# Two half sums for gate and up at the start of a one-core encoder step, with a hand-set order of the first loads and instructions

## The chip, the cores and the metric

The kernel runs on one core of a Trainium2 chip. The metric is device time in microseconds for one execution. In the profile's words PE is TensorE's matmuls, PEld its weight loads, DVE is VectorE, ACT ScalarE, POOL GpSimd, and SP the queue that issues every DMA here.

## The reference

One layer of a streaming encoder is applied to 1024 prompt frames and 32 sample frames, each of 1024 features. The part that matters here is its beginning:

```
mod = silu(c) @ w_mod + b_mod                 # 9 pieces of 1024: shift, scale, gate for three sub-layers
h = rmsnorm(x, gains[0]) * (1 + sc1) + sh1
x = x + 0.5 * g1 * rmsnorm(swiglu(h, w1_gate, w1_up, w1_down), gains[1])
swiglu(h) = (silu(h @ w_gate) * (h @ w_up)) @ w_down          # inner width 2816
```

After it come two attention mixers (a chunk band with 8 heads, and a sliding window with sinks), their output projection, and a second feed-forward block of the first one's form. All is in float32.

## The kernel before

The 1056 frames are cut into three **token blocks** of 384, 384 and 288 columns; features lie on the partitions, in 8 tiles of 128 (`KT`). Every float32 matrix product is made in three: weights and activations are each split into a high part (rounded to fp32r) and the remainder, and `mm3` (lines 325 to 327) adds high x high, high x low and low x high. A weight tile is loaded raw into one of three buffers (`rpool`) and split by ACT (line 303) and DVE (line 304) into one of eight buffers (`wpool`).

The inner width of the feed-forward block is 22 **units** of 128 columns, taken two at a time. For each pair and each block `up` makes gate and up of a unit (2 x 24 products), then silu on ACT (line 550), the product on DVE (551), and the split of the result (553, 554). `down` makes 48 products of a pair into `dn` and adds them to `facc`. For block 0 of the first pair `down` follows at once, since nothing has been begun; then come block 1's gate and up.

Ahead of that stands the **start**. `load_x` fetches a block of x; `transpose_x` turns it by PE (line 617) into a two-bank PSUM buffer, of which there are two (`ps2`), and copies each half out, first DVE, then ACT (line 619). `mod_chunk(n)` loads 2 MB of `w_mod`, makes 512 columns of the modulation (line 186), copies them (`mr`, 189), transposes them (192), and `coefs` adds the bias and makes the scale (`acoef`, 207). Chunks 0 and 1 are the shift of features 0 to 511 and 512 to 1023, chunks 2 and 3 the scale of the same halves. `norm_h` squares x (364), adds up over the features (368, 370, then 357 on PE), takes a reciprocal root by three Newton steps (334 to 338), spreads it over the partitions by PE (`pr`, 405) and makes `h_hi` and `h_lo`. For block 0 (`ahead` is 4) x times the root is made before the coefficients are known (423), and shift and scale come with lines 440 to 442. For blocks 1 and 2 both are in one (420 and 444 to 449). The order in which these pieces are written is the string

```
START = "x02nw1y3"
```

(x a step of block 0, digits chunks, n its norm up to "ahead", w unit 0's gate and up weights, y the load of block 1's x). SP's queue keeps the written order up to the end of the first pair; the other engines' orders are set by a scheduler. Each engine runs its queue in order, so a waiting instruction holds up all that is behind it.

Two small things of later stages stand in the start too: the sinks' loads (lines 276 and 279) and the DVE steps `nsk` (282) and `es` (884) that read them. SP has eight lanes of DMAs, and each DMA waits for the one eight before it.

Of the kernel before, what the change touches and what calls it, by code (L numbers as in the profile page):

```python
# [16 lines left out]
D = 1024  # L17
KT = D // 128
# [36 lines left out]
INORDER = True  # L55
START = "x02nw1y3"
ROUNDS = {"h1": ((), 3), "h3": ((((0, 1), 2), ((2,), 2)), 0)}
# [17 lines left out]
def encoder_step(ctx: ExitStack, tc, x_prompt, x_sample, cache_a_k, cache_a_v, cache_b_k, cache_b_v,  # L75
# [39 lines left out]
    def p1(name, shape=(128, 512)):  # L115
        return ps1.tile(list(shape), F32, name=name, tag="p1")
# [181 lines left out]

    def split_w(src):
        r = rpool.tile([128, 8, 128], F32, name="raw", tag="r")  # L300
        dma.dma_start(r, src)
        w = wpool.tile([128, 2, 8, 128], F32R, name="w", tag="w")
        ae.activation(w[:, 0], r, AF.Copy)  # L303
        ve.tensor_sub(w[:, 1], r, w[:, 0])  # L304
        return w

    def split_cols(wm, c):
        return split_w(wm[0, :, 128 * c:128 * c + 128].rearrange("(k p) n -> p k n", p=128))

# [85 lines left out]

    def mean_rstd(src, kts, w, scale, ends, bank=None):

        bank = bank or pc
        pss = yield from sumsq(src, kts, w, bank, ends)
        y = rstd_cols(pss, w, scale)  # L400
# [100 lines left out]
    def need(key):  # L501
        while key not in done:
            step(1)

    def between(f, tb, j, H):
# [18 lines left out]

    def ffn(key, H, F, wg, wu, wd, per_group, key_out, after, beside=lambda ff, tb: None):
        late, pre = [], {}
# [6 lines left out]

        load(0, 0)
        yield
        for r, (gi, blocks) in enumerate(plan):
# [3 lines left out]
            def up(ff, tb):  # L540
                need((key, tb))
                w = TB[tb][1]
                hi, lo = H[tb]
                ps = [p1("gate"), p1("up")]
                for s in range(2):
                    for k in range(KT):
                        mm3(ps[s][:, :w], wgu[ff][s], k, hi[:, k, :], lo[:, k, :], k == 0, k == KT - 1)
                    step(FAST if gi == 0 else PACE)
                sl = s_tile([128, 384], "sl")
# [39 lines left out]
            if r:  # L589
                load(r, x)  # L590
            load(r, y)
            if r == XAT and key == "h1":
                XIN[1] = load_x(1)
            wgu.update({x: pre[r, x], y: pre[r, y]})
            for ff in grp:
                wds[ff] = split_rows(wd, ff)
            for tb in blocks:
# [41 lines left out]

    ffn1 = ffn("h1", H1, F1, w1_gate, w1_up, w1_down, mod_rest, "h2", lambda tb: between(F1[tb], tb, 0, H2))  # L640
    first = start(0)
    for o in START:
        if o == "x":
            next(first)
        elif o == "n":
            for said in first:
                if said == "ahead":
                    break
        elif o == "w":
            next(ffn1)  # L650
        elif o == "y":
            XIN[1] = load_x(1)
        else:
            mod_chunk(int(o))
    for tb in range(3):
        begin(("h1", tb), start(tb) if tb else first)
    for _ in ffn1:
# [698 lines left out]
```

## Time and profile before

| | |
|---|---|
| median of 3 runs | 2217.93 us (2214.45 to 2221.46) |
| the profiled execution | 2217.6 us, of which the span is 2215.8 |
| mean granted TensorE clock | 0.984 |
| PE busy | 2161.6 us, 98% of the span |
| PE busy in the first 45 us | 28.35 us |
| DVE busy, ACT busy | 1239.1 us, 697.8 us |
| DMA moved | 186.03 MB, 318 GB/s in the first 45 us |

The span is what the trace shows, from the first to the last instruction; 1.8 us lie around it. All times of rows are microseconds from the span's start. A timeline row has start, duration, engine, line, operation, output <- inputs, shapes, and in brackets the idle time before it and what ended it. A row "x4" holds four instructions. In a row of groups stand busy time, mean nanoseconds of one, and idle time before with its releasers. A matmul's own duration covers its passage through the array; the next one starts earlier, so the distance of two starts is what one costs in a row of them.

### The profile page before, as it was taken

The numbers are of one execution on the slowest core, as the hardware profiler recorded it, in microseconds if no ns is written. First come the engines' busy times: TensorE is split into PE (matmuls) and PEld (weight loads), VectorE is DVE, ScalarE is ACT, GpSimd is POOL, SyncE is SP. The second block draws the span as 40 slices with busy tenths as digits, with TensorE's granted clock in tenths as the row PEclk, the third lists the DMA queues.
The fourth block names the chain that finished last, engine by engine and source line by source line (L and its number), as shares of the span: only waits on it lengthen the run. The fifth ranks groups of instructions, "written<-read, shape, count | busy, mean of one in ns | idle before, by whom it ended". The sixth has DMA issues, their size and how long they took to land.

```text
span 2215.8 us, 33976 instructions
## 1 busy us (share of the span) xinstructions
PE 2161.6 (98%) x14012; PEld 2068.6 (93%) x14012; DVE 1239.1 (56%) x2425; ACT 697.8 (31%) x1450; POOL 179.2 (8%) x281
## 2 busy tenths in 40 slices
PE   6999999999999999899999899999999999999998
PEld 4999999999999999799787589999999999999998
DVE  5788667874333497677444865785333333333336
ACT  4411111111121253576444663542111111111133
POOL 1100000000000023001110313220000000000000
PEclk8999999999999999899999899999999999999999
DMA  9253334434122352111112121424211111111122
GB/s 323 93 153 118 111 96 124 143 101 129 39 66 69 101 184 93 38 39 30 50 30 62 46 77 67 134 86 120 66 58 39 57 39 39 58 38 58 39 69 79
DMA packets 200623, 186.03 MB, mean 84 GB/s; under 512 B 7597, under 2 KB 169813, under 8 KB 199317
## 3 DMA queue, kind: packets, MB, share of 16 engines
q1 hardware_dynamic: 200468, 183.87, 27.1%
q8 instruction: 110, 1.80, 0.3%
q14 instruction: 45, 0.36, 0.1%
HBM read 164.12 MB, written 22.86 MB: 84 GB/s over the span
## 4 chain that ended last, share of the span: by engine, by line
PE 90%; DVE 4%; DMA 3%; ACT 1%; issue 1%; POOL 0%; SPq 0%; ACTq 0%; DVEq 0%; POOLq 0%
PE dn L325 7%; PE dn L326 7%; PE dn L327 7%; PE gate L327 7%; PE gate L326 7%; PE up L327 7%; PE up L326 7%; PE gate L325 7%; PE up L325 7%; PE po L713 3%; PE S L752 2%; PE pq L325 2%; PE pq L327 2%; PE pq L326 2%; DMA raw<-in_w_gate_dram 1%; PE pp L776 1%
## 5 line engine op out<-in xcount | busy, mean ns | idle before, releaser
L326 PE MATMUL gate<-h_lo,w 128*128 128x384 f32 (+1 forms) x1056 | 340.2, 322 | 4.0 <-DVE h_lo L446 4.0
L325 PE MATMUL dn<-gg,w 128*128 128x384 f32 (+1 forms) x1056 | 341.4, 325 | 1.1 <-DVE facc L581 1.0
L581 DVE TENSOR_TENSOR facc<-dn,facc 128x768 f32<-128x768 f32 (+1 forms) x240 | 212.9, 889 | 230.2 <-PE dn L327 229.9
L326 PE MATMUL dn<-gg,w 128*128 128x384 f32 (+1 forms) x1056 | 340.6, 323 | 0.6 <-DVE gg L554 0.6
L325 PE MATMUL gate<-h_hi,w 128*128 128x384 f32 (+1 forms) x1056 | 341.0, 323 | 0.0
L327 PE MATMUL gate<-h_hi,w 128*128 128x384 f32 (+1 forms) x1056 | 340.4, 322 | 0.0
L325 PE MATMUL up<-h_hi,w 128*128 128x384 f32 (+1 forms) x1056 | 340.2, 322 | 0.0
L326 PE MATMUL up<-h_lo,w 128*128 128x384 f32 (+1 forms) x1056 | 340.0, 322 | 0.0
L327 PE MATMUL dn<-gg,w 128*128 128x384 f32 (+1 forms) x1056 | 340.0, 322 | 0.0
L327 PE MATMUL up<-h_hi,w 128*128 128x384 f32 (+1 forms) x1056 | 339.9, 322 | 0.0
L304 DVE TENSOR_TENSOR w<-raw,w 128x1024 fp32r<-128x1024 f32 x187 | 231.5, 1246 | 150.5 <-ACT w L303 150.3
L303 ACT ACTIVATE w<-raw 128x1024 fp32r<-128x1024 f32 x187 | 195.7, 1056 | 266.1 <-PE dn L327 103.5
L550 ACT ACTIVATE sl<-gate 128x384 f32<-128x384 f32 (+1 forms) x132 | 60.9, 462 | 563.9 <-PE gate L327 560.9
L551 DVE TENSOR_TENSOR sl<-sl,up 128x384 f32<-128x384 f32 (+1 forms) x132 | 68.5, 519 | 292.1 <-PE up L327 286.1
L326 PEld LDWEIGHTS gate<-h_lo,w 128*128 128x128 f32 x1056 | 198.6, 188 | 4.6 <-DVE h_lo L446 4.6
L325 PEld LDWEIGHTS dn<-gg,w 128*128 128x128 f32 x1056 | 199.2, 189 | 1.6 <-DVE facc L581 1.2
L326 PEld LDWEIGHTS dn<-gg,w 128*128 128x128 f32 x1056 | 199.2, 189 | 1.0 <-DVE gg L554 0.9
L327 PEld LDWEIGHTS dn<-gg,w 128*128 128x128 f32 x1056 | 199.1, 189 | 0.0
L325 PEld LDWEIGHTS gate<-h_hi,w 128*128 128x128 f32 x1056 | 198.7, 188 | 0.1
L327 PEld LDWEIGHTS gate<-h_hi,w 128*128 128x128 f32 x1056 | 198.7, 188 | 0.0
L327 PEld LDWEIGHTS up<-h_hi,w 128*128 128x128 f32 x1056 | 198.7, 188 | 0.0
L325 PEld LDWEIGHTS up<-h_hi,w 128*128 128x128 f32 x1056 | 198.5, 188 | 0.0
(224 smaller groups left out, 3367.4 us busy)
## 6 DMA issues: line engine op xcount, KB each, us to landing
raw<-in_w_mod_dram SPq DMA_DIRECT2D x56, 512.0 KB, 4.0
raw<-in_w_gate_dram SPq DMA_DIRECT2D x54, 512.0 KB, 4.0
raw<-in_w_up_dram SPq DMA_DIRECT2D x54, 512.0 KB, 4.7
raw<-in_w_down_dram SPq DMA_DIRECT2D x54, 512.0 KB, 4.5
raw<-in_w_in_dram SPq DMA_DIRECT2D x18, 512.0 KB, 4.3
wm<-in_w_mod_dram SPq DMA_DIRECT2D x8, 1024.0 KB, 7.4
raw<-in_w_out_dram SPq DMA_DIRECT2D x13, 512.0 KB, 4.5
xr<-xs SPq DMA_DIRECT2D x16, 384.0 KB, 3.5
```

The source lines that it names most:

```text
L303: ae.activation(w[:, 0], r, AF.Copy)
L304: ve.tensor_sub(w[:, 1], r, w[:, 0])
L325: te.matmul(ps, w[:, 0, k], hi, start=start, stop=False)
L326: te.matmul(ps, w[:, 0, k], lo, start=False, stop=False)
L327: te.matmul(ps, w[:, 1, k], hi, start=False, stop=stop)
L550: ae.activation(sl[:, :w], ps[0][:, :w], AF.Silu)
L551: ve.tensor_tensor(sl[:, :w], sl[:, :w], ps[1][:, :w], op=OP.mult)
L581: ve.tensor_tensor(o, ps[:, :, :w], o, op=OP.add)
L713: te.matmul(po[64 * h:64 * h + 64, :n], vsl(j, h, kn), PT(h, j, kn), start=j == 0, stop=j == nt - 1)
L752: te.matmul(S[:, c:ce], self.T[:, h, :], KQ[:, 0, 128 * k0 + c:128 * k0 + ce], start=True, stop=True)
L776: te.transpose(pp[:, j - j0, :], P[:, 128 * j:128 * j + 128], ident)
```

## The change

Six things are done.

- `START` goes. In its place stands a hand-written order, inside a region in which PE, DVE and ACT keep the written order of the region's instructions. SP keeps it as before.
- Loading and using are taken apart: `mod_load` beside `mod_chunk`, `raw_w` beside `split_raw`.
- For block 0 and the first two units, gate and up are made in two halves of the features by `half_products`: features 0 to 511 as soon as chunks 0 and 2 are known, 512 to 1023 after chunks 1 and 3. Unit 0 has two `p1` banks for its sums, unit 1 one of the two `p2` buffers (`gu`). Within a half the three products of each feature tile are sorted by kind.
- Chunk 1 and unit 1's gate weights are loaded ahead of the sinks.
- The squares of block 0 aren't folded on POOL and DVE any more (`fold=not ahead`); PE adds up all eight tiles (24 small matmuls in place of 6).
- Block 1's transposes and the first pair's down weights are written at the end of the region.

```
+    def half_products(ps, ws, h, half):
+        w = TB[0][1]
+        hi, lo = h
+        ks = range(4 * half, 4 * half + 4)
+        for s in range(2):
+            for k in ks:
+                te.matmul(ps[s][:, :w], ws[s][:, 0, k], hi[:, k, :], start=k == 0, stop=False)
+            for k in ks:
+                te.matmul(ps[s][:, :w], ws[s][:, 1, k], hi[:, k, :], start=False, stop=False)
+            for k in ks:
+                te.matmul(ps[s][:, :w], ws[s][:, 0, k], lo[:, k, :], start=False, stop=k == KT - 1)
...
-    def mod_chunk(n):
+    def mod_load(n):
         raws = []
         for g in range(2):
             r = wpool.tile([128, 4, 512], F32, name="wm", tag="w")
             dma.dma_start(r, w_mod[0, 512 * g:512 * (g + 1), 512 * n:512 * (n + 1)]
                           .rearrange("(k p) n -> p k n", p=128))
             raws.append(r)
+        return raws
+
+    def mod_chunk(n, raws):
...
-    def split_w(src):
+    def raw_w(src):
         r = rpool.tile([128, 8, 128], F32, name="raw", tag="r")
         dma.dma_start(r, src)
-        w = wpool.tile([128, 2, 8, 128], F32R, name="w", tag="w")
+        return r
+
+    def split_raw(r, pool=None):
...
         ae.activation(w[:, 0], r, AF.Copy)
         ve.tensor_sub(w[:, 1], r, w[:, 0])
         return w
...
-        r = yield from mean_rstd(x, range(KT), w, 1.0 / D, JN)
+        r = yield from mean_rstd(x, range(KT), w, 1.0 / D, JN, fold=not ahead)
...
-    def ffn(key, H, F, wg, wu, wd, per_group, key_out, after, beside=lambda ff, tb: None):
+    def ffn(key, H, F, wg, wu, wd, per_group, key_out, after, beside=lambda ff, tb: None, halves=False):
...
-        load(0, 0)
-        yield
+        pss, ahead_d = [], {}
+        if halves:
+            raw = [raw_w(cols_of(m, 0)) for m in (wg, wu)]
+            yield
+            raw.append(raw_w(cols_of(wg, 1)))
+            yield
+            for ff in range(2):
+                ws = []
+                for i in range(2):
+                    ws.append(split_raw(raw.pop(0)))
+                    if (ff, i) == (0, 0):
+                        raw.append(raw_w(cols_of(wu, 1)))
+                    yield
+                pre[0, ff] = ws
+                if ff:
+                    gu = p2("gu")
+                    pss.append([gu[:, 0], gu[:, 1]])
+                else:
+                    pss.append([p1("gate"), p1("up")])
+                half_products(pss[ff], ws, H[0], 0)
+                yield
+            for ff in range(2):
+                ahead_d[ff] = split_rows(wd, ff)
+            yield
...
             def up(ff, tb):
+                if pss:
+                    ps = pss.pop(0)
+                    half_products(ps, wgu[ff], H[0], 1)
+                    step(2 * FAST)
...
     first = start(0)
-    for o in START:
...
+    mods = {n: mod_load(n) for n in (0, 2)}
+    next(ffn1)
+    mods[1] = mod_load(1)
+    next(ffn1)
+    with tc.manual_schedule(engines={mybir.EngineType.PE, mybir.EngineType.DVE, mybir.EngineType.Activation}):
+        for _ in range(3):
+            next(first)
+        mod_chunk(0, mods[0])
+        for said in first:
+            if said == "ahead":
+                break
+        mod_chunk(2, mods[2])
+        next(ffn1)
+        next(first)
+        next(first)
+        next(ffn1)
+        mods[3] = mod_load(3)
+        XIN[1] = load_x(1)
+        next(first)
+        next(first)
+        next(ffn1)
+        mod_chunk(1, mods[1])
+        for _ in range(3):
+            next(ffn1)
+        mod_chunk(3, mods[3])
+        run_out(first)
+        second = start(1)
+        for _ in range(3):
+            next(second)
+        next(ffn1)
+    done.add(("h1", 0))
```

How the instructions move is seen in each engine's own order. The first place is SP's queue from unit 0's up weights on (`wm` is a tile of a modulation chunk, `raw` a raw weight, `sk` and `sks` the sinks). Before:

```order
L301 DMA raw<-in_w_up_dram 128x8x128
L276 DMA sk<-in_sinks_b_dram 128x8
L279 DMA sks<-in_sinks_b_dram 32x4x1 x2
L1046 DMA cbv<-in_cache_b_v_dram 128x128
L179 DMA wm<-in_w_mod_dram 128x4x512 x2
L130 DMA X<-in_x_prompt_dram 128x3x1024
L179 DMA wm<-in_w_mod_dram 128x4x512 x2
L301 DMA raw<-in_w_gate_dram 128x8x128
L301 DMA raw<-in_w_up_dram 128x8x128
L301 DMA raw<-in_w_down_dram 128x1024 x2
```

And in the changed kernel:

```order
L303 DMA raw<-in_w_up_dram 128x8x128
L178 DMA wm<-in_w_mod_dram 128x4x512 x2
L303 DMA raw<-in_w_gate_dram 128x8x128
L278 DMA sk<-in_sinks_b_dram 128x8
L281 DMA sks<-in_sinks_b_dram 32x4x1 x2
L1127 DMA cbv<-in_cache_b_v_dram 128x128
L303 DMA raw<-in_w_up_dram 128x8x128
L178 DMA wm<-in_w_mod_dram 128x4x512 x2
L129 DMA X<-in_x_prompt_dram 128x3x1024
L303 DMA raw<-in_w_down_dram 128x1024 x2
```

Chunk 1 and unit 1's gate have moved ahead of the sinks, unit 1's up weights ahead of chunk 3, and block 1's x behind chunk 3.

The second place is DVE's queue around the coefficients of chunk 2 (the second `modT` pair; `w` is the split of a weight). Before:

```order
L194 TENSOR_REDUCE modT<-pmt 128x2x4
L203 TENSOR_TENSOR modT<-modT,cst 128x2x4
L304 TENSOR_TENSOR w<-raw,w 128x1024
L282 TENSOR_SCALAR nsk<-sk 128x8
L884 TENSOR_SCALAR es<-sks 64x1
L194 TENSOR_REDUCE modT<-pmt 128x2x4
L203 TENSOR_TENSOR modT<-modT,cst 128x2x4
L207 SCALAR_TENSOR_TENSOR acoef<-modT,cst 128x2x4
L368 TENSOR_TENSOR sq<-sq 128x384 x2
L370 TENSOR_TENSOR sq<-sq 128x384
```

And in the changed kernel, from block 0's scaled x on:

```order
L437 TENSOR_TENSOR n<-xt,pr 128x768 x4
L284 TENSOR_SCALAR nsk<-sk 128x8
L965 TENSOR_SCALAR es<-sks 64x1
L196 TENSOR_REDUCE modT<-pmt 128x2x4
L205 TENSOR_TENSOR modT<-modT,cst 128x2x4
L209 SCALAR_TENSOR_TENSOR acoef<-modT,cst 128x2x4
L312 TENSOR_TENSOR w<-raw,w 128x1024
L455 TENSOR_SCALAR n<-n,acoef,modT 128x384
L456 TENSOR_TENSOR h_lo<-n,h_hi 128x384
L455 TENSOR_SCALAR n<-n,acoef,modT 128x384
L312 TENSOR_TENSOR w<-raw,w 128x1024
```

The norm of block 0, up to the four scaled tiles, now stands ahead of chunk 2's coefficients, and the first weight's split behind them.

The third place is ACT's queue from the copies of block 1's transposes to the splits of the first down weights. Before:

```order
L619 COPY xt<-pt 128x4x128
L364 ACTIVATE sq<-xt 128x768 x3
L303 ACTIVATE w<-raw 128x1024
L440 ACTIVATE h_hi<-n,modT,acoef 128x384 x4
L364 ACTIVATE sq<-xt 128x768
L619 COPY xt<-pt 128x4x128 x2
L619 COPY xt<-pt 128x4x32
L550 ACTIVATE sl<-gate 128x384
L553 ACTIVATE gg<-sl 128x384
L550 ACTIVATE sl<-gate 128x384
L303 ACTIVATE w<-raw 128x1024 x2
```

And in the changed kernel:

```order
L454 ACTIVATE h_hi<-n,modT,acoef 128x384 x4
L681 COPY xt<-pt 128x4x128
L611 ACTIVATE sl<-gate 128x384
L614 ACTIVATE gg<-sl 128x384
L681 COPY xt<-pt 128x4x128
L611 ACTIVATE sl<-gu 128x384
L614 ACTIVATE gg<-sl 128x384
L681 COPY xt<-pt 128x4x128
L311 ACTIVATE w<-raw 128x1024 x2
L378 ACTIVATE sq<-xt 128x768 x4
L681 COPY xt<-pt 128x4x128 x2
```

Block 1's copies and squares stood ahead of block 0's silu; now the copies stand between and the squares behind it. On PE the transposes of the sample rows and the first column sums of block 1 now stand ahead of the first down product, and all 24 of the first half of the down products ahead of block 1's `pr`, where 6 stood before.

More of the change, by code (lines that the diff above doesn't have):

```diff
@@ L394, in encoder_step, with mean_rstd @@
     waits = [0]
-    def mean_rstd(src, kts, w, scale, ends, bank=None):
+    def mean_rstd(src, kts, w, scale, ends, bank=None, fold=True):
         bank = bank or pc
-        pss = yield from sumsq(src, kts, w, bank, ends)
+        pss = yield from sumsq(src, kts, w, bank, ends, fold)
         y = rstd_cols(pss, w, scale)
@@ L503, in need, with run_out @@
             step(1)
+    def run_out(gen):
+        for _ in gen:
+            pass
     def between(f, tb, j, H):
@@ L590, in ffn @@
                 load(r, x)
-            load(r, y)
+            if r or not halves:
+                load(r, y)
             if r == XAT and key == "h1":
@@ L638, in mod_rest @@
             begin("bias", bias_rows())
-    ffn1 = ffn("h1", H1, F1, w1_gate, w1_up, w1_down, mod_rest, "h2", lambda tb: between(F1[tb], tb, 0, H2))
+    ffn1 = ffn("h1", H1, F1, w1_gate, w1_up, w1_down, mod_rest, "h2", lambda tb: between(F1[tb], tb, 0, H2),
+               halves=True)
     first = start(0)
-    for o in START:
-        if o == "x":
-            next(first)
[L645 to L649, printed above, removed]
-            next(ffn1)
[L651 to L656, printed above, removed]
+    mods = {n: mod_load(n) for n in (0, 2)}
[4 more added lines that the diff above has]
+        for _ in range(3):
+            next(first)
+        mod_chunk(0, mods[0])
[14 more added lines that the diff above has]
+        for _ in range(3):
+            next(ffn1)
+        mod_chunk(3, mods[3])
[5 more added lines that the diff above has]
+    done.add(("h1", 0))
+    for tb in (1, 2):
+        begin(("h1", tb), second if tb == 1 else start(tb))
     for _ in ffn1:
```

29 lines of the change are left out of this document (20 added, 9 removed).

## The prediction

> **What bounds the kernel now.** I read the page's part 1, then the busy time by stretches, then the timeline of the first 80 us engine by engine.
>
> ```profile
> span 2215.8 us, 33976 instructions
> core 0: us, PE busy (x) PEld busy (x) DVE busy (x) ACT busy (x) POOL busy (x), PEclk, DMA share, GB/s
> 0.00:45.00 45.00, 28.35 (x143) 14.83 (x144) 19.62 (x45) 15.78 (x24) 5.82 (x10) 0.85 0.93 318
> 45.00:72.00 27.00, 26.74 (x173) 25.99 (x171) 22.11 (x44) 17.81 (x30) 6.37 (x6) 1.00 0.93 322
> 72.00:80.00 8.00, 6.17 (x27) 5.93 (x26) 8.00 (x11) 4.54 (x9) 3.81 (x4) 0.79 0.01 2
> 80.00:860.00 780.00, 778.25 (x4972) 776.61 (x4971) 492.15 (x798) 172.33 (x274) 30.02 (x25) 1.00 0.35 105
> ```
>
> PE idles 16.65 us of the first 45 and 1.83 around 73; from 80 to 860 it is busy without a break. So an edit of the start is worth what it moves the moment R at which PE is next fed without a gap, once the same products are done. The timeline gives it:
>
> ```profile
> 45.55 0.42 PE L325 MATMUL gate<-h_hi,w 128*128 128x384 f32 x1
> 48.86 0.99 DVE L207 SCALAR_TENSOR_TENSOR acoef<-modT,cst 128x8 f32<-128x8 f32 x1
> 50.94 2.50 ACT L440 ACTIVATE h_hi<-n,modT,acoef 128x384 fp32r<-128x384 f32 x4
> 67.70 0.83 PE L405 MATMUL pr<-ident,ry 128*128 128x128 f32 x6
> 68.66 4.29 DVE L420 SCALAR_TENSOR_TENSOR n<-xt,acoef,pr 128x384 f32<-128x384 f32 x8
> 71.73 0.34 PE L325 MATMUL up<-h_hi,w 128*128 128x384 f32 x1
> 71.90 0.34 PE L325 MATMUL gate<-h_hi,w 128*128 128x384 f32 x1
> 74.07 0.45 PE L326 MATMUL gate<-h_lo,w 128*128 128x384 f32 x1 [1.83 <-DVE h_lo L446]
> ```
>
> Two moments matter. T = 49.85 (48.86 + 0.99): the scale of the second half of the features is ready. R = 74.07: the first low part of block 1 is ready, 24.2 after T and 6.37 after the start of `pr` (67.70). At R, all of block 0's gate and up, 24 of its down products and three of block 1's are done. In the new order the same stand before that wait, so R can be compared. A product takes 0.17 (71.90 less 71.73).
>
> The old order uses the wait for T already: 36 of the 96 products of block 0's first two units (the first half of the features of three of the four sums) stand between 45.55 and T's `h_hi`. The new one puts 48 there. The gain in products is 12 x 0.17 = 2.1 us, but 16 of block 1's 24 transposes, done before T until now, come after it.
>
> **Part 1, up to T.**
>
> ```profile
> 16.37 0.60 ACT L189 ACTIVATE mr<-pm 128x512 f32<-128x512 f32 x1 [1.37 <-PE pm L186]
> 22.21 3.03 ACT L364 ACTIVATE sq<-xt 128x768 f32<-128x768 f32 x4
> 54.43 0.72 PE L357 MATMUL pss<-ones,sq 128*128 128x1 f32 x6
> 30.92 0.16 DVE L391 TENSOR_SCALAR rv<-pss 128x3 f32<-128x3 f32 x1 [2.14 <-PE pss L357]
> 32.89 0.16 DVE L338 SCALAR_TENSOR_TENSOR ry<-rt,ry 128x3 f32<-128x3 f32 x1
> 35.15 3.55 DVE L423 TENSOR_TENSOR n<-xt,pr 128x768 f32<-128x768 f32 x4 [2.10 <-PE pr L405]
> 24.60 0.14 DVE L884 TENSOR_SCALAR es<-sks 64x1 f32<-64x1 f32 x1 [1.43 <-DMA sks<-in_sinks_b_dram]
> 25.00:30.00 5.00, 3.78 (x13) 2.10 (x13) 3.71 (x6) 1.19 (x2) 1.09 (x2) 0.50 1.06 402
> 14.35 1.93 PE L186 MATMUL pm<-wm,csil 128*32 128x512 f32 x16 [0.70 <-ACT csil L166]
> 17.02 0.66 PE L192 MATMUL pmt<-ident,mr 128*128 128x128 f32 x4 [0.74 <-ACT mr L189]
> ```
>
> Nothing changes to 16.97 (first `mr`). Then the squares, first in line now, take 3.03, to 20.0. Without the fold three adds on POOL and three on DVE go, and the sums are 24 matmuls in place of 6; the row of six records is three of them, so 8 times 0.72 = 5.8 us from 17.8, to 23.6. The root takes 2.13 (30.92 to 33.05), to 25.7; `pr` 0.83; the four `n` 3.55, to 30.1. Chunk 2's product can start on PE at 26.5: 1.93, `mr` 0.60, `pmt` 0.66, so 29.7.
>
> Next on DVE, ahead of chunk 2's coefficients, stands `es`, which waits for the sinks' small loads. Before, these followed the first up weights, and `es` ran at 24.60. Now two tiles of chunk 1 and a gate weight are queued before them: 2.6 MB at 402 GB/s (row 25 to 30) is 6.5 us, so 31.1. The coefficients follow by about 32.5 (30.7 if the sinks come early).
>
> ```profile
> L303 ACT ACTIVATE w<-raw 128x1024 fp32r<-128x1024 f32 x187 | 195.7, 1056 | 266.1 <-PE dn L327 103.5
> L304 DVE TENSOR_TENSOR w<-raw,w 128x1024 fp32r<-128x1024 f32 x187 | 231.5, 1246 | 150.5 <-ACT w L303 150.3
> L441 DVE TENSOR_SCALAR n<-n,acoef,modT 128x384 f32<-128x384 f32 x8 | 4.1, 565 | 0.0
> L442 DVE TENSOR_TENSOR h_lo<-n,h_hi 128x384 fp32r<-128x384 f32 x4 | 2.2, 545 | 0.0
> L442 POOL TENSOR_TENSOR h_lo<-n,h_hi 128x384 fp32r<-128x384 f32 x4 | 4.7, 1169 | 16.3 <-DVE n L441 16.3
> ```
>
> From there DVE is a queue: split of gate 0 (1.25) to 33.7; 0.57 + 0.55 + 0.57 for the first two features, to 35.4; split of up 0, to 36.7; 1.7 for the next two, to 38.4; POOL's 1.17, to 39.6. PE's gate half ends there and the up half (12 x 0.17) runs to 41.8. Only then come chunk 1 (1.93; 43.7) and its `mr` (44.3). Behind `mr` on ACT stand the splits of unit 1: gate 1 on ACT 1.06, then two DVE splits of 1.25, to 47.9. PE's last 8 products of unit 1's half end at 49.3; chunk 3 (1.93), `mr`, `pmt` and the small DVE steps (1.0) give T = 53.5.
>
> The split of gate 0 also releases SP: the load of up 1 waits for its raw buffer, and chunk 3's two loads, X of block 1 and the down weights stand behind it. From 33.7, 2.6 MB at 402 GB/s take 6.5 us: with some 2 us of start, chunk 3 lands near 42, hidden under the 49.3 at which PE turns to it. If DVE got there 7 us faster, that load would be next.
>
> ```profile
> 76.14 0.52 PE L325 MATMUL gate<-h_hi,w 128*128 128x384 f32 x1
> 76.46 0.52 PE L325 MATMUL dn<-gg,w 128*128 128x384 f32 x1
> ```
>
> After the 1.83 us gap the products run at 0.32 (76.46 less 76.14) with PEclk 0.79 from 72 to 80. The new PE queue has gaps as long between 24 and 39, so I take one stretch at half speed on the path, 1.5 us: T = 55. Bounds: 51.7 (sinks early, full speed) and 57.5 (up half and chunk 1 both at half speed). Against 49.85 that is +5.2 (+1.9 to +7.7).
>
> The Trainium skill (TensorE: Matmul & The Clock Gate, What's actually happening) says that the clock halves after at least one idle window of about 3.4 us. By it a gap of 1.83 us need not cost anything, T would be 53.5 and the sum 2229.5; the trace shows the half speed after that gap, so I don't follow it here.
>
> **Part 2, from T to R.**
>
> ```profile
> L619 DVE COPY xt<-pt 128x512 f32<-128x512 f32 x8 | 5.4, 685 | 11.3 <-PE pt L617 11.3
> L619 ACT COPY xt<-pt 128x512 f32<-128x512 f32 x8 | 4.7, 582 | 11.4 <-DVE xt L619 11.3
> L550 ACT ACTIVATE sl<-gate 128x384 f32<-128x384 f32 x2 | 1.0, 481 | 0.5 <-PE gate L327 0.5
> L551 DVE TENSOR_TENSOR sl<-sl,up 128x384 f32<-128x384 f32 x2 | 1.1, 551 | 0.1
> L553 ACT ACTIVATE gg<-sl 128x384 fp32r<-128x384 f32 x2 | 1.0, 524 | 3.5 <-DVE sl L551 3.5
> L554 DVE TENSOR_TENSOR gg<-sl,gg 128x384 fp32r<-128x384 f32 x2 | 1.1, 558 | 0.6 <-ACT gg L553 0.6
> 44.26 1.09 PE L617 MATMUL pt<-ident,X 128*128 128x128 f32 x8
> 58.49 0.68 PE L617 MATMUL pt<-ident,raw 32*128 32x32 f32 x8
> raw<-in_w_up_dram SPq DMA_DIRECT2D x54, 512.0 KB, 4.7
> ```
>
> Times after T. Four `h_hi` take 2.5; PE's remaining 26 products to the end of unit 0 end at 7.1. ACT's queue now has block 1's copies behind unit 0's silu: silu 0.48, product 0.55, `gg` 0.52 and 0.56, second tile's copies 0.69 and 0.58: 10.7. Its third tile's transposes wait for that buffer, as `gu` holds the other of the two: 1.09, then 0.69 and 0.58 (and unit 1's silu beside them): 13.1. ACT then splits both down weights (2.1), squares block 1 (3.03) and copies a tile of block 2 (0.58): 18.8. PE stands still until that copy, since the transposes of the sample rows need its buffer and all down products are queued behind: 0.68, sums 0.72, 11 down products 1.9, sums: 22.8.
>
> DVE has the splits of the next unit's gate and up ahead of the root. The up load can be issued only when the second down split (17.3) has freed its buffer: 4.7 to land, ACT 1.06, DVE 1.25 give 24.3. Root 2.1 to 26.4, and 6.37 from `pr` to R: 32.8. Against 24.2 that is +8.6. Bounds: +7.1 (that load not in the way: root from 22.8) and +10.6 (load 2 us late). Before, block 1's squares began at 47.8 and 18 down products still lay behind `pr`; this cover is gone.
>
> Behind R the work is the same. Sum: 5.2 + 8.6 = 13.8 on the profiled execution's 2217.6 (2217.93 is the median): 2231. The scheduler also reorders some rows near the end of attention; no row prices that, I put 0 with 2 us to either side.
>
> **Rivals.** *Faster:* PE's 16.65 idle us take the products and block 1 stays hidden. R must then lie under 67.4. After T, PE itself needs 48 products (8.3), 40 transposes (4 x 1.09 + 0.68 = 5.0), 24 down products (4.1) and the sums (1.4), 18.8 in all, so T must fall to 48.6 with no wait for block 1 at all; at T = 47, R is 65.8, which gives 2209. For it: the idle time, and loads no longer held up behind the small ones. Against it: the DVE queue of part 1. Chance 0.10.
>
> *Within 0.3%:* T = 51.7, and block 1's chain 4 us shorter than I make it (loads landing early, ACT's order looser): R = 80.5, and 2224 is the border of this case; its middle is near 2221. Chance 0.17.
>
> *Still slower, by the clock:* PE gets its work in pieces of about 2 us with gaps from 24 to T, as between 25 and 30, where PEclk was 0.50 with PE busy for 3.78 of 5. If all of it runs at half speed, the up half, chunk 1, the last products and chunk 3 add 2.1 + 1.9 + 1.4 + 1.9 and the second halves another 1.7 to the 53.5: T = 62.5, 2239. Chance 0.12. The same section of the Trainium skill (TensorE: Matmul & The Clock Gate) bears on this: it takes about 3.4 us of sustained work to release the clock, which pieces of 2 us never give. The row of 25 to 30 agrees.
>
> **How the numbers follow.** My forecast has 0.61: +9.0 to +18.3, so 2226.6 to 2236. With the clock's case slower has 0.73, same 0.17, faster 0.10; 0.3% (6.7 us) is about what a measurement of this kernel can tell from no change. The range of 2219 to 2240 takes in the clock's case and the middle of the second; the faster case and some of the tails are left out.
>
> **What would show it.** Right: `es` near 31, the split of gate 0 right behind it, chunk 3's scale near 55, a PE gap of some 5 us ahead of the sample rows' transposes, and block 1's first low part near 88. Wrong: `es` before 27, chunk 3's scale before 50, or down products without a gap behind the transposes.

## The result and the profile after

The changed kernel takes 2238.88 us (median of 4 runs, 2234.24 to 2242.43), the kernel before, run beside it, 2216.19 (2211.42 to 2221.46). The ratio is 1.0105 (95% interval 1.0090 to 1.0120): slower by 1%. The profiled execution of the changed kernel took 2237.62 us; its span is 2235.8, 20.0 more than before's; the medians are 22.7 apart.

The busy time by stretches, in the columns of the prediction (busy time of each engine, granted TensorE clock, DMA share, GB/s):

```profile
0.00:45.00 45.00, 30.09 (x140) 22.36 (x141) 14.75 (x37) 13.09 (x19) 3.36 (x7) 0.73 0.80 269
45.00:72.00 27.00, 23.49 (x151) 18.08 (x151) 11.12 (x21) 9.51 (x16) 2.20 (x2) 1.00 0.56 205
72.00:80.00 8.00, 3.24 (x22) 2.87 (x22) 7.32 (x8) 5.63 (x9) 4.12 (x3) 0.69 0.93 301
80.00:100.00 20.00, 15.26 (x58) 14.74 (x59) 14.81 (x30) 9.80 (x17) 4.39 (x5) 0.70 0.45 150
```

PE is busier than before up to 45 us (30.09 for 28.35), but at a clock of 0.73 in place of 0.85: part of that busy time is the same work, slower. Between 45 and 100 PE idles 13 us, where it idled 2.1 before. From 100 on it is busy without a break, as before.

Rows of the timeline from the first column sums to T (the scale of the second half of the features):

```profile
17.71 7.91 PE L371 MATMUL pss<-ones,sq 128*128 128x1 f32 x48
29.48 3.64 PE L188 MATMUL pm<-wm,csil 128*32 128x512 f32 x16
33.20 0.14 DVE L965 TENSOR_SCALAR es<-sks 64x1 f32<-64x1 f32 x1
35.48 0.17 DVE L209 SCALAR_TENSOR_TENSOR acoef<-modT,cst 128x8 f32<-128x8 f32 x1
45.80 1.92 PE L188 MATMUL pm<-wm,csil 128*32 128x512 f32 x16
54.47 1.92 PE L188 MATMUL pm<-wm,csil 128*32 128x512 f32 x16
58.29 0.17 DVE L209 SCALAR_TENSOR_TENSOR acoef<-modT,cst 128x8 f32<-128x8 f32 x1
```

T is 58.46, 8.6 later than before. `es` has no bracket: it waited for nothing. Chunks 1 and 3 (45.80, 54.47) stand behind the half sums, as the written order has them.

And rows from T to R (the first low part of block 1):

```profile
68.70 0.58 ACT L681 COPY xt<-pt 128x512 f32<-128x512 f32 x1 [1.35 <-DVE xt L681]
73.58 3.03 ACT L378 ACTIVATE sq<-xt 128x768 f32<-128x768 f32 x4
77.13 1.06 PE L679 MATMUL pt<-ident,raw 32*128 32x32 f32 x8 [4.21 <-ACT xt L681]
83.70 1.27 PE L371 MATMUL pss<-ones,sq 128*128 128x1 f32 x6
87.48 0.16 DVE L352 SCALAR_TENSOR_TENSOR ry<-rt,ry 128x3 f32<-128x3 f32 x1
88.97 0.83 PE L419 MATMUL pr<-ident,ry 128*128 128x128 f32 x6
91.24 0.45 PE L339 MATMUL gate<-h_hi,w 128*128 128x384 f32 x1 [1.44 <-ACT h_hi L458]
95.34 0.51 PE L340 MATMUL gate<-h_lo,w 128*128 128x384 f32 x1 [3.31 <-DVE h_lo L460]
```

R is 95.34, 21.3 later than before (74.07), 12.7 of them behind T. PE stands still for 4.21 us ahead of the sample rows' transposes, and for 1.44 and 3.31 behind `pr`, where before it waited 1.83. The span grew by 20.0, so a little over 1 us came back behind R.

### The profile page after: what moved, and what is told of

Read it like the earlier page. It is cut to its first block, busy times and chain, and to the rows that moved or that the text cites. A ratio compares the mean times of both kernels' runs of the same rounds, so it can differ in the third digit from the quotient of the medians.

```text
span 2235.8 us, 34033 instructions
## 1 busy us (share of the span) xinstructions
PE 2171.8 (97%) x14048; PEld 2080.0 (93%) x14048; DVE 1236.7 (55%) x2422; ACT 696.5 (31%) x1450; POOL 177.5 (8%) x278
## 4 chain that ended last, share of the span: by engine, by line
PE 90%; DVE 4%; DMA 2%; ACT 1%; issue 1%; POOL 1%; SPq 0%; ACTq 0%; POOLq 0%; DVEq 0%
PE dn L339 7%; PE dn L341 7%; PE dn L340 7%; PE gate L341 7%; PE up L340 7%; PE gate L340 7%; PE up L341 7%; PE up L339 7%; PE gate L339 7%; PE po L794 3%; PE S L833 2%; PE pq L339 2%; PE pq L341 2%; PE pq L340 2%; PE wo L339 1%
## 5 line engine op out<-in xcount | busy, mean ns | idle before, releaser
L340 PE MATMUL gate<-h_lo,w 128*128 128x384 f32 (+1 forms) x1040 | 334.4, 322 | 5.5 <-DVE h_lo L460 5.5
L339 PE MATMUL gate<-h_hi,w 128*128 128x384 f32 (+1 forms) x1040 | 335.3, 322 | 1.4 <-ACT h_hi L458 1.4
L341 PE MATMUL gate<-h_hi,w 128*128 128x384 f32 (+1 forms) x1040 | 334.7, 322 | 0.0
L340 PE MATMUL up<-h_lo,w 128*128 128x384 f32 (+1 forms) x1040 | 334.4, 322 | 0.0
L339 PE MATMUL up<-h_hi,w 128*128 128x384 f32 (+1 forms) x1040 | 334.3, 321 | 0.0
L341 PE MATMUL up<-h_hi,w 128*128 128x384 f32 (+1 forms) x1040 | 333.9, 321 | 0.0
L339 PEld LDWEIGHTS gate<-h_hi,w 128*128 128x128 f32 x1040 | 195.5, 188 | 1.7 <-ACT h_hi L458 1.6
L341 PEld LDWEIGHTS up<-h_hi,w 128*128 128x128 f32 x1040 | 195.6, 188 | 0.0
L341 PEld LDWEIGHTS gate<-h_hi,w 128*128 128x128 f32 x1040 | 195.5, 188 | 0.0
L340 PEld LDWEIGHTS up<-h_lo,w 128*128 128x128 f32 x1040 | 195.4, 188 | 0.0
```

What stands on the lines that cost most here:

```text
L339: te.matmul(ps, w[:, 0, k], hi, start=start, stop=False)
L340: te.matmul(ps, w[:, 0, k], lo, start=False, stop=False)
L341: te.matmul(ps, w[:, 1, k], hi, start=False, stop=stop)
```

## The experiments

My theory at the start: the written order of the queues costs the time, T by chunks 1 and 3 behind the half sums, R by block 1's copies and squares behind block 0's silu. The rivals: the half sums themselves, the loads behind the blocked SP queue, and the half clock of PE. All times in the table are from one profile each; "time" and ratio are from all runs beside the kernel before. R of the two kernels with the cover put back is left out, since fewer down products lie ahead of it there.

| kernel | T | `pr` | R | R less T | time | ratio to before |
|---|---|---|---|---|---|---|
| before | 49.85 | 67.70 | 74.07 | 24.2 | 2216.19 | |
| changed | 58.46 | 88.97 | 95.34 | 36.9 | 2238.88 | 1.0105 (1.0090 to 1.0120) |
| scheduler's order | 56.78 | 80.55 | 86.92 | 30.1 | 2228.78 | 1.0065 (1.0043 to 1.0088) |
| chunks ahead | 55.46 | 88.76 | 95.19 | 39.7 | 2234.33 | 1.0086 (1.0068 to 1.0103) |
| squares folded | 54.32 | 83.58 | 90.02 | 35.7 | 2230.97 | 1.0074 (1.0059 to 1.0089) |
| 20 idle products | 57.64 | 89.14 | 95.51 | 37.9 | 2238.01 | 1.0100 (1.0084 to 1.0115) |
| 6 idle products | 59.37 | 87.53 | 93.97 | 34.6 | 2232.85 | 1.0079 (1.0065 to 1.0092) |
| loads ahead | 58.10 | 86.83 | 93.28 | 35.2 | 2235.16 | 1.0100 (1.0081 to 1.0119) |
| block 1 ahead | 58.22 | 89.73 | 96.10 | 37.9 | 2239.74 | 1.0108 (1.0094 to 1.0121) |
| all repairs | 48.01 | 76.54 | 82.92 | 34.9 | 2226.66 | 1.0050 (1.0038 to 1.0063) |
| repairs and cover | 41.36 | 62.41 | | | 2215.52 | 0.9993 (0.9985 to 1.0002) |
| before, x behind chunk 3 | 48.59 | 69.94 | 76.31 | 27.7 | 2219.53 | 1.0015 (1.0005 to 1.0025) |
| scheduler and fold | 55.05 | 77.79 | 84.16 | 29.1 | 2225.97 | 1.0046 (1.0031 to 1.0061) |
| cover, copies ahead | 40.73 | 66.52 | | | 2218.59 | 1.0015 (1.0004 to 1.0025) |

Runs of one kernel scatter by some 4 us to either side, so moments of a profile tell more than a median's last digit. The moments scatter too: in the changed kernel and the three whose order up to T is its own (20 and 6 idle products, block 1 ahead), T lies between 57.6 and 59.4.

### The order given back to the scheduler

```
-    with tc.manual_schedule(engines={PE, DVE, Activation}):
+    with ExitStack():
```

> The half sums, the order of the loads and the unfolded squares stay as in the changed kernel; only the fixed order of PE, DVE and ACT in the start region is given back to the scheduler. My theory is that the fixed order of the queues costs the time: the scheduler puts the second chunk's small steps ahead of the split of up 0, chunk 1's and chunk 3's steps ahead of the splits of unit 1, and block 1's copies and squares among block 0's silu. Then the scale of the second half of the features (T, 58.5 us in the changed kernel) comes near 52, and the first low part of block 1 (R, 95.3) near 82: about 2225 us, 13 below the changed kernel. Rival, the half sums themselves or the order of the loads cost it: T stays within 2 us of 58.5 and the time stays near 2238. Rival, the half sums are worth something once the order is free: R under 74 and a time under 2217.

R came 8.4 us earlier and the time 10: the largest gain of a single edit at R (in the time it can't be told from that of the fold below, since their intervals overlap). That is the theory's side, though T fell by 1.7 only, as the first rival had it, and R less T by 6.8. So here the order costs more behind T than ahead of it. No R under 74: in this order the half sums gained nothing.

### Chunks 1 and 3 ahead

```
         mod_chunk(2, mods[2])
+        mod_chunk(1, mods[1])
...
-        mod_chunk(1, mods[1])
+        mod_chunk(3, mods[3])
         for _ in range(3):
             next(ffn1)
-        mod_chunk(3, mods[3])
```

> Chunk 1's products, copy and transposes are written right behind chunk 2's, and chunk 3's right ahead of the split of unit 1's gate weights; nothing else changes. If T (58.5) is late because chunks 1 and 3 stand in PE's queue behind the half sums and in ACT's behind the splits of unit 1, chunk 3 comes as soon as its load has landed (45.8): T near 50, R near 87, about 2230 us. If the half clock of PE sets T, the work ahead of it is the same and T stays over 55; if the late load of chunk 3 set it, T cannot come ahead of 49.

Rows of this kernel's timeline:

```profile
48.71 1.48 PE L552 MATMUL up<-h_hi,w 128*128 128x384 f32 x4
49.99 1.48 PE L554 MATMUL up<-h_lo,w 128*128 128x384 f32 x4
51.40 1.98 PE L188 MATMUL pm<-wm,csil 128*32 128x512 f32 x16
95.19 0.69 PE L340 MATMUL gate<-h_lo,w 128*128 128x384 f32 x1 [3.30 <-DVE h_lo L460]
```

T was 55.46, not 50: chunk 3 waited for no load, but for unit 0's 24 products, which ran at half speed (four in 1.28 us from 48.71 to 49.99). That is what the clock's theory had said. And R did not move at all: unit 1's first half, 24 products, had only gone to the other side of T. So T alone does not set R, which my theory had taken for granted; the time, 4.6 us lower by the medians, has an interval that overlaps the changed kernel's.

### The squares folded again

```
-        r = yield from mean_rstd(x, range(KT), w, 1.0 / D, JN, fold=not ahead)
+        r = yield from mean_rstd(x, range(KT), w, 1.0 / D, JN)
```

> The squares of block 0 are folded on POOL and DVE again, so that 6 column sums stand in PE's queue in place of 24; all else is as in the changed kernel. In the changed kernel the sums end about 25.6. By the half clock's theory 24 sums take 7.9 us since they wait for ACT's squares and run slowly; folded, the root comes no earlier than before's (the adds took 1.2 us each on POOL), so I expect T and R within 1.5 us of the changed kernel's 58.5 and 95.3 and the time near 2238. Rival, the unfolded sums delay the norm of block 0: T falls by 2 to 3 us, and the time to 2235.

My expectation was wrong and the rival right, by more than it said: T 4.1 and R 5.3 earlier, the time 8 us lower. The sums and the clock of this kernel:

```profile
21.00 2.72 PE L371 MATMUL pss<-ones,sq 128*128 128x1 f32 x12 [3.38 <-POOL sq L384]
32.00:38.00 6.00, 3.52 (x10) 2.76 (x11) 5.87 (x10) 3.45 (x5) 1.91 (x1) 0.82 0.58 180
```

The sums ended 1.9 us earlier (23.72 for 25.62), and from 32 to 38 the clock was 0.82, where the changed kernel had 0.50 (its row stands below): this goes with the other 2.2 us of T, though no run changed the clock alone there. 54.3 lies outside the scatter of T given above.

### Products into the gap, 20 and 6

```
+        warm = p1("warm")
+        for _ in range(20):        # 6 in the second
+            te.matmul(warm[:, :384], ident, XT[0][:, 0, :], start=True, stop=True)
```

> 20 products of 384 columns into a bank that nothing reads are added on PE at the end of the start region, ahead of the transposes of the sample rows, where PE idles 4.2 us in the changed kernel; their result is used nowhere. By the clock's theory the down products behind run at 0.17 in place of 0.32 us each: 13 of them stand between the second column sums and the spreading of the root, so R falls from 95.3 to about 92 or 93, and the time to about 2235. If the gap ahead of block 1's low part (1.4 and 3.3 us) sets the end in any case, or if the clock does not come back, R stays within 1 us of 95.3 and the time near 2238.

```profile
69.44 13.07 PE L737 MATMUL warm<-xt,ident 128*128 128x384 f32 x40
89.14 0.83 PE L419 MATMUL pr<-ident,ry 128*128 128x128 f32 x6
```

The 20 took 13.07 us, 0.65 each, as products of plain float32: they filled three times the gap. The down products behind did run at 0.17, but they began 7 us late, 12 of the 24 now stood behind `pr`, and R stayed. So this run tells little about the clock; the second was made for it.

> As the run with products that nothing reads, but 6 of them in place of 20: those were full float32 and took 13.1 us in all, 0.65 each, and so filled far more than the gap of 4.2 us. Six take 3.9 us and keep PE busy from 72.9 to about 76.8. By the clock's theory the transposes of the sample rows, the sums and the down products then run at full speed: the 24 down products take 4.2 us in place of 8.3, the root's spreading (pr, 88.97 in the changed kernel) comes near 87.7, right behind the root, and R near 94. So I expect no more than 1.3 us of the 12.7 that part 2 lost from the clock there, and a time within 2 us of 2238. Rival, the clock's half speed is what part 2 lost: R under 91.

```profile
71.16 4.04 PE L737 MATMUL warm<-xt,ident 128*128 128x384 f32 x12
78.03 0.68 PE L679 MATMUL pt<-ident,raw 32*128 32x32 f32 x8 [1.09 <-ACT xt L681]
82.42 0.53 PE L339 MATMUL dn<-gg,w 128*128 128x384 f32 x1
82.75 0.53 PE L340 MATMUL dn<-gg,w 128*128 128x384 f32 x1
87.53 0.91 PE L419 MATMUL pr<-ident,ry 128*128 128x128 f32 x6 [1.01 <-DVE ry L352]
```

`pr` and R came where expected (87.5 and 94.0), and `pr` now waits 1.01 us for the root. R fell by 1.4 us, and by 2.3 counted from T, which was 0.9 later here. That is not all that the clock can cost: behind waits of 1.09 and 0.46 us it was halved again from 80.5 to 83.4 (0.33 from 82.42 to 82.75), so nine of the down products ahead of the last sums still went at half speed, which I estimate at nine times 0.15, another 1.4 us. The rival's R under 91 did not come. The time fell by 6 us, of which R explains 1.4; the rest is behind R or scatter, and stays open.

### The loads ahead

```
+    mods[3] = mod_load(3)
+    XIN[1] = load_x(1)
     with tc.manual_schedule(engines={PE, DVE, Activation}):
...
-        mods[3] = mod_load(3)
-        XIN[1] = load_x(1)
```

> Chunk 3 and block 1's x are loaded right behind unit 1's gate weights, ahead of the sinks and of unit 1's up weights, so that DMA has no empty stretch of 8 us; the order on PE, DVE and ACT stays as in the changed kernel. Chunk 3 then lands near 35 in place of 45.8. By my theory T waits for PE's order and not for a load: T and R counted from block 0's sums stay within 1.5 us (T 32.8 after the sums, R 69.7 after them), the time near 2238. Rival, the blocked SP queue costs the time: T comes 4 us earlier or more, and R with it, under 2234.

```profile
17.57 6.59 PE L371 MATMUL pss<-ones,sq 128*128 128x1 f32 x48
57.93 0.17 DVE L209 SCALAR_TENSOR_TENSOR acoef<-modT,cst 128x8 f32<-128x8 f32 x1
86.83 0.91 PE L419 MATMUL pr<-ident,ry 128*128 128x128 f32 x6 [0.44 <-DVE ry L352]
```

The sums ended 1.5 us earlier here, and T 0.4: counted from the sums it is later by 1.1. The other 1.7 us of R go with the clock: the down products behind the last sums started 0.17 apart (84.14, 84.32) where the changed kernel had 0.32, and `pr` waited for the root. So without any product in the gap R less T moved nearly as far as with the 6 idle products, and a single profile can't tell the two apart. The blocked SP queue and DMA's empty stretch cost T next to nothing, since PE's order is later.

### Block 1 ahead

```
         mod_chunk(3, mods[3])
+        second = start(1)
+        for _ in range(3):
+            next(second)
         run_out(first)
-        second = start(1)
-        for _ in range(3):
+        for _ in range(2):
             next(second)
```

> Block 1's three transposes with their copies are written right behind chunk 3, ahead of the second half of block 0's features, and two of its four squares right behind those; all else is as in the changed kernel. By my theory part 2 lost its 12.7 us since block 1's copies and squares stand behind block 0's two silu steps and the down splits: T stays near 58.5, the second half of block 0 comes some 3 us later, but the root of block 1 no longer waits for it: R falls from 95.3 to 87 to 90 and the time to about 2231. Rival, PE's own work after T (and its half clock) sets R: moving the same work gives nothing and R stays over 94.

My theory failed here: R 96.10, the time the same.

```profile
59.87 1.09 PE L679 MATMUL pt<-ident,X 128*128 128x128 f32 x8 [1.40 <-ACT xt L681]
76.70 0.73 PE L371 MATMUL pss<-ones,sq 128*128 128x1 f32 x6
83.88 0.16 DVE L352 SCALAR_TENSOR_TENSOR ry<-rt,ry 128x3 f32<-128x3 f32 x1
89.73 0.83 PE L419 MATMUL pr<-ident,ry 128*128 128x128 f32 x6
```

Block 1's last sums came 7.0 us earlier (76.70 for 83.70) and its root 3.6 (83.88 for 87.48), yet `pr` 0.8 later. The root gained less than the sums, since DVE had two splits of weights ahead of it and began it at 80.45. All 24 down products stand ahead of `pr` on PE, and they wait for block 0, which this edit delayed: with one buffer free each tile takes 2.5 us, as ACT's copy waits for DVE's and the next tile for both. So the second thing that holds R is the place of the down products ahead of `pr`.

### All repairs, and the cover put back

The first kernel has the fold, chunk 3's load ahead of the region, and this order in it:

```
+    mods[3] = mod_load(3)
...
         mod_chunk(0, mods[0])
-        for said in first:
-            if said == "ahead":
-                break
+        for _ in range(4):
+            next(first)           # squares
+        next(ffn1)                # split of gate 0
+        XIN[1] = load_x(1)
+        next(first)               # root, pr
+        next(ffn1)                # split of up 0
+        next(first)               # scaled x
         mod_chunk(2, mods[2])
...
+        mod_chunk(1, mods[1])     # between h of tiles 0, 1 and 2, 3
...
+        for _ in range(3):
+            next(ffn1)            # unit 0's first half, splits of unit 1
         mod_chunk(3, mods[3])
...
+        next(ffn1)                # unit 1's first half, behind block 1's transposes
+        for _ in range(2):
+            next(second)          # squares of block 1
         next(ffn1)                # down splits
```

> All repairs in one, with the half sums kept: squares of block 0 folded again; chunk 3 and block 1's x loaded ahead of the sinks; unit 0's splits around block 0's root, where DVE waits; chunk 1 right behind chunk 2; unit 1's splits ahead of chunk 3, chunk 3 ahead of unit 1's half sums; block 1's transposes among the second half of block 0's features, two of its squares behind them. If the written order, and not the half sums, costs the time, T comes near 44 (the kernel before: 49.9) and R near 64 to 68 (before: 74.1): 2208 to 2212, faster than both. Rival, the half clock: PE still works in pieces up to T, so T is 47 to 50 and R over 72, about 2216. Rival, the half sums cost by themselves: R over 78 and the time over 2220.

```profile
47.84 0.17 DVE L209 SCALAR_TENSOR_TENSOR acoef<-modT,cst 128x8 f32<-128x8 f32 x1
72.75 0.16 DVE L352 SCALAR_TENSOR_TENSOR ry<-rt,ry 128x3 f32<-128x3 f32 x1
76.54 0.83 PE L419 MATMUL pr<-ident,ry 128*128 128x128 f32 x6
82.92 0.69 PE L340 MATMUL gate<-h_lo,w 128*128 128x384 f32 x1 [3.31 <-DVE h_lo L460]
```

T fell by 10.5 us, below that of the kernel before, R by 12.4 and the time by 12. But R is over the 78, and the time over the 2220, that I had given to the half sums. Here is why I don't put it to them: the root ends at 72.91, and `pr` starts only at 76.54, behind the last of 24 down products; 3.31 us of idle PE follow, as in the changed kernel. The second kernel changes that: chunk 3 moves ahead of unit 0's first half, and the second halves and `pr` are written in the region too; besides, the second halves are made in two steps, gate and up.

```
+        mod_chunk(3, mods[3])     # ahead of unit 0's first half
...
+        next(ffn1)                # unit 0's second half, gate
+        next(second)              # block 1's third tile
+        next(ffn1)                # unit 0's second half, up
...
+        next(ffn1)                # unit 1's first half
+        for _ in range(3):
+            next(second)          # squares 3 and 4, sums, root
+        next(ffn1)                # down splits
+        next(ffn1)                # unit 1's second half, gate
+        next(second)              # pr
+        next(ffn1)                # unit 1's second half, up
```

> As the run with all repairs, with three things more, both half sums kept: chunks 2, 1 and 3 stand behind each other, ahead of unit 0's first half, as chunk 3 lands near 34; unit 0's second half and block 1's three transposes stand ahead of unit 1's halves, so that block 1's squares and root come early; and the spreading of block 1's root (pr) stands ahead of the last 12 products of unit 1 and of all 24 down products, which lie behind it again as cover. In the run with all repairs T was 48.0 and R 82.9, since 24 down products, half of them at half speed, stood between block 1's root and pr, and PE then waited 1.4 and 3.3 us. If that lost cover is what is left of part 2, T comes near 39, pr near 57 to 60, and the time is 2208 to 2214, at or under the kernel before. Rival, the half clock or DVE's load (copies, splits, silu, root within 15 us) takes it back: pr over 66 and a time over 2217.

```profile
40.48 0.94 PE L550 MATMUL gate<-h_hi,w 128*128 128x384 f32 x4
41.19 0.17 DVE L209 SCALAR_TENSOR_TENSOR acoef<-modT,cst 128x8 f32<-128x8 f32 x1
62.41 0.83 PE L419 MATMUL pr<-ident,ry 128*128 128x128 f32 x6
69.27 0.53 PE L339 MATMUL dn<-gg,w 128*128 128x384 f32 x1 [2.06 <-DVE sl L617]
```

T 41.36, `pr` 62.41, and the time that of the kernel before (0.9993, 0.9985 to 1.0002), with all half sums in place: 23 us below the changed kernel. So the order of instructions and loads, with the fold, can make up the whole loss without giving up the half sums. Three things moved at once from the first of these kernels to the second, so their shares are not told apart. The gain that I had expected (2208 to 2214) did not come: T is 8.5 us and `pr` 5.3 us ahead of the kernel before, and the time is the same. Where that went is not shown. Nor was this order tried without the half sums, so it is open whether they cost something that the earlier chunk 3 pays for. A gain of theirs is not to be seen here: the first half's products begin at 40.48, within 1 us of the moment at which the second half's scale is known, so there is nothing left to run ahead of.

### Two smaller moves

The first is one letter in the kernel before, the second a shift in the last kernel:

```
-START = "x02nw1y3"
+START = "x02nw13y"
```

```
+        for _ in range(2):
+            next(second)          # tiles 0 and 1 of block 1
         next(ffn1)                # splits of unit 1
         next(ffn1)
-        for _ in range(2):
-            next(second)
```

> The kernel before with one letter moved: block 1's x is loaded behind chunk 3 and not ahead of it; no half sums. Chunk 3 (1.6 MB less ahead of it, at 390 GB/s) lands 4 us earlier. If T is bounded by that load in the kernel before, T falls from 49.9 to about 46, and R by 2 to 4 us (block 1's transposes now wait for its x instead): 2213 to 2215 beside 2215 to 2217. Rival, R is bounded by PE's products or by block 1's norm: nothing, or a loss of some us since block 1's x comes later and its norm with it.

```profile
36.34 2.49 PE L186 MATMUL pm<-wm,csil 128*32 128x512 f32 x16
40.86 1.97 PE L617 MATMUL pt<-ident,X 128*128 128x128 f32 x16 [2.02 <-DMA X<-in_x_prompt_dram]
42.66 0.60 PE L192 MATMUL pmt<-ident,mr 128*128 128x128 f32 x4
```

The rival was right: chunk 3's products ran 4 us earlier, but the scheduler put block 1's transposes, which now wait for their x, ahead of chunk 3's transposes (`pmt`), and three splits ahead of its scale. T fell by 1.3, and R came 2.2 later, since block 1's norm came later.

> The last kernel with the half sums, with one move: block 1's first two tiles are transposed and copied ahead of the splits of unit 1's weights on ACT and DVE, where the copies waited 3 us (DVE 45.6 to 48.7) and PE 1.3. If what is left there is again a matter of the written order, block 1's squares and pr come 1.5 to 2 us earlier and the time falls by 1 to 2 us to 2213 or 2214, just under the kernel before, which no interval here would tell from it with certainty. Rival, PE is the bound from 41 us on: the same time as without the move, 2215.5.

```profile
33.80 16.15 SPq L303 DMA_DIRECT2D raw<-in_w_down_dram  x2
50.00 0.43 SPq L129 DMA_DIRECT2D X<-in_x_prompt_dram  x1
58.13 1.24 PE L684 MATMUL pt<-ident,X 128*128 128x128 f32 x8 [2.88 <-DMA X<-in_x_prompt_dram]
```

Both theories missed: it is some 3 us slower. The later split frees its raw buffer later, SP waits with the second down load until then, and block 2's x, queued behind, is issued at 50.00 in place of 47.22. PE waits 2.88 us for it, and from 60 to 72 the mean clock is 0.76, where the kernel without the move had 0.89.

### The scheduler's order with the fold

The first and the third edit together.

> Half sums and order of the loads as in the changed kernel, squares of block 0 folded again, and the order of PE, DVE and ACT left to the scheduler. Apart, the folding took 5.3 us off R (95.3 to 90.0) and the scheduler 8.4 (to 86.9). If they are two losses, R comes near 82 and the time near 2224; if the scheduler's order already covers the unfolded sums (the root came 0.5 us earlier there), R stays near 86 and the time near 2228. By either it stays slower than the kernel before, since the loads stay in the changed order and the down products ahead of block 1's root.

R came out at 84.16, between the two expectations, and the two times' intervals overlap. Whether these are two losses or one is not settled.

## Why the prediction came out as it did

**Direction and mechanism held.** Slower, by queues in which block 1 and the chunks stand behind block 0's half sums, within the range (2219 to 2240). The size was short: 13.8 us forecast, 21.3 at R, 20.0 in the span. The forecast's own bounds end at 2236, and both parts ran over theirs; 2238.88 lies within the range because this was stretched for the clock's case, which is luck as far as the sum goes. Of the signs, the gap ahead of the sample rows' transposes came as said (4.21 us for some 5), `es` at 33.20 for 31, but for another reason; chunk 3's scale (58.3) and the first low part of block 1 (95.3) were late.

**Part 1 was +8.6 in place of +5.2, over its bound of +7.7.** The step that failed is the one on `es`: DMA had moved everything asked for by 30 us, the sinks' loads among it, `es` ran at 33.20 without a wait, behind `n`, and held nobody. The step on the 24 column sums was mis-sized: 7.91 us, not 5.8. What came late in place of `es` is chunk 2 on PE, 3.64 us where I took 1.93, so its scale stood at 35.48, not 32.5. The order of the rest was as written: chunk 1 at 45.80, chunk 3 at 54.47, its load not in the way (the run with the loads ahead showed that). The rows put the size down to the clock: I put 1.5 us of half speed on the path, and it was halved from 21 to 44 us. `pr` took 1.62 us and not 0.83, chunk 2 3.64 where chunk 1, later and at full clock, took 1.92, and the sums 2.1 more than in my sum. The run with the fold took 4.1 of the 8.6 back, but it also left out most of the sums, so the clock's share by itself is not shown.

**Part 2 was +12.7 in place of +8.6, over its bound of +10.6.** Up to the copy of block 2's tile it held to the letter: unit 0's products ended 7.2 us after T (7.1), the second tile's copy 10.8 (10.7), the third's 13.3 (13.1). Then the last sums came 26.5 after T and not 22.8: the 11 down products ahead of them ran at 0.32, the transposes took 1.06, not 0.68, and the two rows of sums 1.44 and 1.27, not 0.72. So the up load, forecast as the bound at 24.3, did not hold the root: its split ended at 83.98, before those sums. And 13 more down products at half speed set `pr` 1.3 us behind the root; I had let `pr` follow the root at once, a wait put at nothing, though all 24 stand ahead of it on PE.

**The clock rival** named the measured time (2239) but by another way: the clock was 1.00 from 45 to 72 us, T was 58.5 and not 62.5, and more than half of the loss lay behind T. Behind T the runs with 6 idle products and with the loads ahead, in which the clock came back sooner, were 2.3 and 1.7 us shorter from T to R; ahead of T its share was not tried apart from the fold.

**What I had not seen** is that neither T nor block 1's sums set R by themselves once `pr` is late. Chunks ahead: T less by 3.0, R the same. Block 1 ahead: its sums earlier by 7.0, R no better. All repairs, T less by 10.5: R less by 12.4, and `pr` still 3.6 us behind the root. Only with `pr` ahead of the down products as well did the time come back to that of the kernel before.

## What to carry to other kernels

A reordering that starts one block sooner must be read to the point where the next block's chain joins: here the products that used to cover block 1's norm had come to stand ahead of it. In a written order a chain is freed only when every queue on it is: moving the chunks took 3.0 us off T, moving block 1 took 7.0 off its sums, and neither moved R; the repairs together took 12 us off the time, and with `pr` ahead of the down products 23. And before work is split to fill a wait for data, ask whether the data could come first: with chunk 3 loaded earlier the half sums had nothing left to run ahead of.

## What the runs showed of the hardware

The column sums did not hold the clock up. Stretches of the changed kernel, then of the kernel with the loads ahead:

```profile
17.00:21.00 4.00, 3.92 (x32) 3.69 (x32) 0.36 (x2) 2.85 (x4) 0.00 (x0) 0.93 1.17 313
21.00:26.00 5.00, 4.62 (x22) 4.53 (x22) 0.31 (x2) 0.00 (x0) 0.00 (x0) 0.50 1.07 376
32.00:38.00 6.00, 3.52 (x14) 1.29 (x6) 4.18 (x11) 3.86 (x6) 0.00 (x0) 0.50 0.01 2
```

```profile
17.00:21.00 4.00, 3.92 (x35) 3.69 (x34) 0.36 (x2) 2.71 (x4) 0.00 (x0) 1.00 1.17 312
21.00:26.00 5.00, 3.16 (x19) 3.07 (x18) 1.49 (x10) 0.00 (x0) 0.00 (x0) 0.58 1.06 377
```

In the changed kernel PE is busy for 3.92 of 4 us and then without a gap until the sums end at 25.62, and the granted clock falls from 0.93 to 0.50. The matmuls are of one column each; that this is why they don't hold the clock is my reading, and no run tried it. The moment at which the clock falls differs from profile to profile, so the same 48 records took 6.59, 7.91 and 9.29 us in three kernels with the same order of PE up to there (loads ahead, changed, 6 idle products), and chunk 2 began at 28.02, 29.48 and 30.88. At T the three are only 1.3 us apart. The Trainium skill (TensorE: Matmul & The Clock Gate, What's actually happening) has the clock released by about 3.4 us of sustained busy time, and halved after an idle window as long; here it is halved in the midst of busy time, so the measurement decides: busy time in the profile is not what the clock goes by. Nor does it need an idle window of that length: 1.83 us before, and 1.09 with 0.46 in the run with 6 products, were each followed by some 3 us of half speed. And the length of one gap does not decide it, as the run with 20 products shows:

```profile
95.51 0.45 PE L340 MATMUL gate<-h_lo,w 128*128 128x384 f32 x1 [2.91 <-DVE h_lo L460]
```

The clock stayed at 1.00 behind this gap of 2.91 us, and the next products started 0.17 apart (95.80, 95.97); behind the gap of 3.31 at the same place the changed kernel's started 0.32 apart. What else sets the moment is not shown.

In the run with 20 products, a product of 384 columns of plain float32 took 0.65 us, one of fp32r 0.17.
